# A two-layer decoder trunk: key stage begun later, last triangular inversion spread wider, bonus task later, recurrence hops closer

## The chip, the cores and the metric

The kernel runs on one core of one Trainium2 chip. The metric is the device time of one execution in microseconds (us). Three runs of the kernel before gave 2402.3, 2398.12 and 2408.5 us; their median, 2402.3 us, is the time that the change is held against. The profile was taken of one further execution.

Five engines have a queue of their own and work through it in order: PE (matrix products), DVE (elementwise), ACT (activation functions and copies), POOL (elementwise), and SP, which only issues transfers. PEld is the weight load of PE, which overlaps it.

## What is computed

Layer 0 is an attention with forget gates, layer 1 an RWKV-7 time mixing; each has a modulated norm ahead of it and a gated residual add behind it. The change lies in layer 1. Cut to what matters:

```python
xr, xw, xk, xv, xa, xg = (h + xx * mu[i] for i in range(6))     # xx = h shifted by one token, less h
r, k, v, z = xr @ w_in[0], xk @ w_in[1], xv @ w_in[2], xg @ w_in[3]
w_log = -softplus(-(w0 + tanh(xw @ w1) @ w2)) - 0.5             # low-rank stage: w, a, v
decay = exp(-exp(w_log))
v = v + (v_first - v) * sigmoid(v0 + (xv @ v1) @ v2)
a = sigmoid(a0 + (xa @ a1) @ a2)
kk = normalised(k * k_k);  k = k * (1 + (a - 1) * k_a)
# per head, token by token:  a_t = -kk, b_t = kk * a
S = S * w_t + (S a_t) b_t^T + v_t k_t^T ;   y_t = S r_t
y = groupnorm(y) * lnx_w + lnx_b + sum(r * k * r_k) * v         # the last term is the bonus
x = x + gate * ((y * silu(z)) @ w_out)
```

SEQ is 512, D_MODEL 2048, 32 heads of 64. All is float32; a large product is made of three passes over operands split into a high and a low part.

## The kernel before, in words

**The backbone.** Layer 1 has 74 dense tiles of PE work: 10 left of the keys, then 16 each of receptance (r), values (v), gate (z) and output projection. A tile is one PSUM bank of 128 x 512 outputs and takes 16 k-steps; a step is three matmuls, `pj<-hi,whi`, `pj<-hi,wlo`, `pj<-lo,whi`. Four k-steps use one weight group (256 KB): SP loads it as `raw`, ACT rounds it to `whi`, DVE makes `wlo`. There are three buffers for `raw` and four for `whi` and `wlo`.

**What sets the order.** Everything else runs as tasks: Python generators that emit instructions and then `yield` how much PE work is to pass before they go on. `Flow` (L108) keeps a clock that advances with every matmul emitted (a 128 x 512 matmul by 512/2400 = 0.213), and a heap of due tasks. So the numbers in `yield` fix where an instruction stands in each engine's queue. They set no time: on the chip an engine that reaches an instruction whose input isn't there waits, and all that stands behind it in its queue waits too.

**The side work of layer 1** (`side`, L1758) goes through a low-rank stage (`lora_k`, `lora_up`), then 16 `keys` tasks, one for each 128 rows of keys, KEY = 9.8 apart. A `keys` task loads `ip`, `kt` and `aa`, squares the keys on ACT (`sq<-kt`), splits the square (`mhi` on ACT, `mlo` on DVE) and sums it over a head on PE (`S<-mhi,blkr`, `S<-mlo,blkr`, in `means`, L1097); it goes on to the products that the chunks of 64 tokens need. After each four of them `invert` (L1388) inverts 32 x 32 triangles, 128 at once, in 30 steps of two operations (`lt<-lane`, `lane<-lane,lt`). The first three inversions run on POOL. The last one (group 3, DG) runs on DVE, its steps spread over DINV of PE work; its first step waits for the transfer `lane<-mld`. `inverse` follows DINV + 8 behind it. When all keys are through, the recurrence begins.

**The recurrence.** `stage` (L1477) loads for each of 16 pairs of chunks and makes `eI<-prk` on ACT; `products` (L1529) makes `L` and `GP`, and `recur` (L1590) takes one chunk after the other in three hops, each on the grid of HOP (`hop`, L1585): x from S and L, x from `xs` and `QP`, x from S and `tok`. `bonus` (L1569) is started 2 behind the end of a stage; it loads `vv`, and sums `prk` over a head with the same `means` as the keys (`mhi<-prk`, `mlo<-prk`). `normed` (L1646) norms the outcome of a pair of chunks, with `means` twice (`mhi<-ys`, `mhi<-sq`). All these products share two PSUM banks named S. `gated` multiplies with silu(z), and the output tiles need all of that.

Nearly all instructions pass through one recording helper, so that the profile shows them with its line, L90. They are told apart by the names of what they write and read.

Of the kernel before, what the change touches and what calls it, by code (L numbers as in the profile page):

```python
# [131 lines left out]
def body(ctx, tc, a, out, dbg=None, stop=0):  # L132
# [961 lines left out]
    def read(tag, n):  # L1094
        rings[tag][n] = fl.t + 0.7

    def means(q, w, x, th, tl):  # L1097
        hi = q.tile([P, T], R, tag=th, name="mhi")
        lo = q.tile([P, T], R, tag=tl, name="mlo")
        act_hi(hi, x)  # L1100
        yield 0.6
        dve.tensor_tensor(out=lo, in0=x, in1=hi, op=OP.subtract)
        yield 1.8
        n = yield from need("S")
        ss = bank("S")
        pe.matmul(ss, w, hi, start=True, stop=False)
        pe.matmul(ss, w, lo, start=False, stop=True)
        return ss, n

    def take(tag):  # L1110
        while not free[tag]:
            yield 0.2
        free[tag] -= 1
# [22 lines left out]
    def keep(j, o):  # L1136
        t = mq.tile([P, T], F, tag="z", name="kt")
        act.activation(t, o, AF.Copy)
        yield 1.5
        sp.dma_start(kTd[j], t)  # L1140
# [5 lines left out]
    def lora_k(q, k):  # L1146
        if k == 0:
            lb.extend(bank(t) for t in "SSy")
        hp = load(mq, h1d[k], "hp", (P, T + 1), bufs=NHP)
        raw = load(q, a["lora"][k], "rawl", (P, NL))  # L1150
        yield 4
        wh = q.tile([P, 1, NL], R, tag="whl", name="whl")
        wl = q.tile([P, 1, NL], R, tag="wll", name="wll")
        act_hi(wh[:, 0], raw)
        ns = (1, 4, 3)
        ms = [q.tile([P, T], F, tag=f"m{n}", name="m", bufs=1 + (n == 3)) for n in ns]
        d = q.tile([P, T], F, tag="d", name="d")
        pool.tensor_tensor(out=d, in0=hp[:, 0:T], in1=hp[:, 1:], op=OP.subtract)
        ts = [tuple(q.tile([P, T], R, tag=f"m{x}{n}", name="m" + x) for x in "hl") for n in ns]
        yield 1.4  # L1160
        for i in range(5):
            if i == 1:
                dve.tensor_tensor(out=wl[:, 0], in0=raw, in1=wh[:, 0], op=OP.subtract)
            if i < 3:
                dve.scalar_tensor_tensor(out=ms[i], in0=d,
                                         scalar=vecs[:, V_MU + ns[i], k:k + 1],
                                         in1=hp[:, 1:], op0=OP.mult, op1=OP.add)
            if 1 <= i < 4:
                act_hi(ts[i - 1][0], ms[i - 1])
            if 2 <= i:  # L1170
                e = pool if i - 2 < 1 else dve
                e.tensor_tensor(out=ts[i - 2][1], in0=ms[i - 2], in1=ts[i - 2][0],
                                op=OP.subtract)
            yield 0.7
        yield 1
        sp.dma_start(mxd[0, k], ms[2])
        premixed.add((0, k))
        for t, o, (m0, m1) in ((ts[i], lb[i], lspan[i]) for i in (1, 2, 0)):
            mm3(o[0:m1 - m0, :], (wh, wl), 0, t, k == 0, k == KT - 1, m0, m1)
            yield 1  # L1180
        if k == KT - 1:
            lb.append(None)
# [22 lines left out]
    def lora_w(q, g, n):  # L1205
        nm, rows = (("w2", LW), ("a2", LA_), ("v2", LV))[n]
        raw = load(q, a[nm][:, g * T:(g + 1) * T], "w2r", (rows, T), bufs=3)
        if n == 2:
            wh = q.tile([2 * LV, T], R, tag="v2h", name="v2h", bufs=2)
        else:  # L1210
            wh = q.tile([rows, T], R, tag="w2h", name="w2h", bufs=4)
            wl = q.tile([rows, T], R, tag="w2l", name="w2l", bufs=4)
        yield 6.5
        act_hi(wh[0:rows], raw)
        yield 1.2
        if n == 2:
            dve.tensor_tensor(out=wh[LV:], in0=raw, in1=wh[0:LV], op=OP.subtract)
        else:
            dve.tensor_tensor(out=wl, in0=raw, in1=wh, op=OP.subtract)
        yield 1.2  # L1220
        uw[g, n] = (wh,) if n == 2 else (wh, wl)
# [64 lines left out]
    def mixz(q, k):  # L1286

        yield from take("m")
        hp = load(mq, h1d[k], "hp", (P, T + 1), bufs=NHP)
        yield 5  # L1290
        m = q.tile([P, T], F, tag="mm", name="m", bufs=2)
        act.activation(m, hp[:, 1:], AF.Copy, scale=omu[:, 2, k:k + 1])
        yield 1.5
        dve.scalar_tensor_tensor(out=m, in0=hp[:, 0:T], scalar=vecs[:, V_MU + 5, k:k + 1],
                                 in1=m, op0=OP.mult, op1=OP.add)
        free["m"] += 1
        yield 1.5
        sp.dma_start(mxd[2, k], m)
        premixed.add((2, k))
# [267 lines left out]
        staged[m] = SV, L, qp, gp, dec, tok  # L1567

    def bonus(q, g, u, prk):  # L1569
        vv = q.tile([P, T], F, tag="vv", name="vv", bufs=1)  # L1570
        sp.dma_start(vv.rearrange("p (j t) -> p j t", j=NJ), vvd[g][:, u])
        yield 6
        yield from take("B")
        bo, n = yield from means(q, blkr, prk.rearrange("p j c t -> p (j c t)"), "mh", "ml")
        free["B"] += 1
        yield 0.9
        yield from take("bv")
        bv = q.tile([P, T], F, tag="bv", name="bv", bufs=2)
        dve.scalar_tensor_tensor(out=bv, in0=bo, scalar=float(DH), in1=vv, op0=OP.mult,
                                 op1=OP.mult)  # L1580
        read("S", n)
        free["prk"] += 1
        staged[g, u] = bv

    def hop():  # L1585
        n = fl.t // HOP
        while fl.t // HOP == n:
            yield 0.1
# [162 lines left out]


    STW = 5
    DG, DINV = (3,), 32
    HOP = 3.9
    INV, KEY = 54, 9.8

    def side(q):  # L1758
        for j, o in enumerate(ks):
            fl.start(0, keep(j, o))  # L1760
        for k in range(KT):
            fl.start(fl.t, lora_k(q, k))
            yield 5.2
        while len(lb) < 4:
            yield 0.2
        yield 0.5
        pools.close()
        q = pools.enter_context(tc.tile_pool(name="uq", bufs=2, reuse_waits="tile"))
        for n in range(3):
            fl.start(fl.t, lora_w(q, 0, n))  # L1770
        rmask = q.tile([P, NCH, C], F, name="rmask", bufs=1)
        pool.memset(rmask, 1.0)
        pool.memset(rmask[:, :, 0:1], 0.0)
        rms.append(rmask)
        lora_act(q)
        yield 3.5
        for j in range(KT):
            for n in range(3):
                if j % 4 == 0 and j < KT - 4:
                    fl.start(fl.t, lora_w(q, j // 4 + 1, n))  # L1780
                fl.start(fl.t, lora_up(q, j, n))
                yield 0.8
        while len(ups) < 3 * KT:
            yield 0.2
        yield 3
        pools.close()
        kp = pools.enter_context(tc.tile_pool(name="kp", bufs=1, reuse_waits="tile"))
        eIs.append(kp.tile([P, NCH, C + 1], F, name="eI"))
        for i in range(5):
            qts.append(kp.tile([P, NCH, C], F, name=f"qt{i}"))  # L1790
            for r in (32, 96):
                pool.memset(qts[i][r:r + 32, :, 0:32], 0.0)
        pool.memset(eIs[0][:, :, 0:1], 1.0)
        for j in range(KT):
            if "v" in dbg:
                print("keys", j, fl.t, len(ends))
            fl.start(fl.t, keys(kp, j))
            fl.start(fl.t + 5, mixz(kp, j))
            yield KEY
        while len(qd) < KT or len(premixed) < 3 * KT:  # L1800
            yield 0.2
        yield 3
        pools.close()
        rk = pools.enter_context(tc.tile_pool(name="rk", bufs=1, reuse_waits="tile"))
        for i in range(4):
            QP.append([rk.tile([P, NJ, C], F, name=f"QP{i}{h}") for h in range(2)])
            GP.append([rk.tile([P, NJ, C], F, name=f"GP{i}{h}") for h in range(2)])
            for h in range(2):
                pool.memset(QP[i][h][OS[h]], 0.0)
                pool.memset(GP[i][h][OS[h]], 0.0)  # L1810
        def stages():
            for n in range(NG * NU):
                g, u = divmod(n, NU)
                while any(NJ * g + i not in rd for i in range(NJ)):
                    yield 0.2
                yield from stage(rk, g, u)

        fl.start(fl.t, stages())
        fl.start(fl.t, recur(rk))

    fl.start(0, side(q))
    Av, Ar, Az, G = [], [], [], []
    ready = {(id(A), k) for k in range(KT)}
# [37 lines left out]
```

## Time and profile before

| | |
|---|---|
| median of three runs | 2402.3 us (2398.12 to 2408.5) |
| profiled execution: its time, its span | 2401.73 us, 2399.9 us |
| PE busy | 2302.2 us, 96% of the span |
| PEld, DVE, ACT, POOL busy | 75%, 67%, 52%, 29% |
| granted TensorE clock, mean | 0.982 |

Layer 1 fills about the last 1100 us. A row of a timeline begins with its start and its duration in us; what stands in brackets is how long the engine had been idle before it, and what ended that. A row of windows gives busy time and count for each engine, then the granted clock (PEclk), the busy share of the 16 DMA engines and GB/s.

### The profile page before, as it was taken

To read this page: it belongs to the slowest core of one execution; us is meant where nothing else is said; L and a number is where in the kernel's file an instruction comes from. 1 tells how busy PE (TensorE), PEld (TensorE's weight loads), DVE (VectorE), ACT (ScalarE), POOL (GpSimd) and SP (SyncE) were. 2 spreads that over 40 slices of the span, in tenths; PEclk is the share of its full clock that TensorE was granted. 3 is DMA by queue.
4 is the path that set the end of the run, shared out by engine and by line. 5 is a ranking of instruction groups with operands and counts; after the bars stand their busy time and mean duration, and the time that the engine had idled before them with its cause. 6 is when DMAs were issued, how large, how long until landed. Compare 5 with 4: busy or idle time off the path is not lost. (4 is left out here: it accounts for less than half of the span.)

```text
span 2399.9 us, 39413 instructions
## 1 busy us (share of the span) xinstructions
PE 2302.2 (96%) x13626; PEld 1807.3 (75%) x13626; DVE 1605.2 (67%) x2850; ACT 1256.5 (52%) x2300; POOL 694.4 (29%) x1114
## 2 busy tenths in 40 slices
PE   6999999999999999998999898899999899999999
PEld 4787777877778778886777676677777677777787
DVE  6886778888888635336797567666476776755322
ACT  4435655555565545225646777763345556665221
POOL 0002333442424210110141208771245535450000
PEclk8999999999999999999999999899999999999999
DMA  8864466766666346445756999886867766544543
GB/s 307 328 227 156 128 211 217 222 213 213 205 224 220 114 161 225 142 141 157 223 179 198 308 263 277 256 252 187 233 187 195 219 174 194 167 132 154 161 137 97
DMA packets 388152, 480.23 MB, mean 200 GB/s; under 512 B 146032, under 2 KB 217840, under 8 KB 384112
## 3 DMA queue, kind: packets, MB, share of 16 engines
q1 hardware_dynamic: 386288, 475.08, 63.7%
q0 software_dynamic: 1664, 2.63, 0.3%
q8 instruction: 108, 1.77, 0.3%
q14 instruction: 92, 0.75, 0.1%
HBM read 381.63 MB, written 95.95 MB: 199 GB/s over the span
## 5 line engine op out<-in xcount | busy, mean ns | idle before, releaser
L90 PE MATMUL pj<-hi,whi 128*128 128x512 f32 x2416 | 987.4, 409 | 11.0 <-ACT hi L90 8.2
L90 PE MATMUL pj<-hi,wlo 128*128 128x512 f32 x2416 | 959.4, 397 | 10.1 <-DVE wlo L90 10.0
L90 PE MATMUL pj<-lo,whi 128*128 128x512 f32 x2416 | 959.9, 397 | 0.0
L90 DVE TENSOR_TENSOR wlo<-raw,whi 128x512 fp32r<-128x512 f32 (+2 forms) x628 | 473.4, 761 | 255.1 <-ACT whi L90 252.4
L90 ACT ACTIVATE whi<-raw 128x512 fp32r<-128x512 f32 (+2 forms) x628 | 393.9, 634 | 399.0 <-PE pj L90 215.1
L90 PEld LDWEIGHTS pj<-hi,whi 128*128 128x128 f32 x2416 | 459.5, 190 | 116.8 <-ACT hi L90 9.2
L90 PEld LDWEIGHTS pj<-lo,whi 128*128 128x128 f32 x2416 | 458.3, 190 | 108.4 <-DVE lo L90 0.7
L90 PEld LDWEIGHTS pj<-hi,wlo 128*128 128x128 f32 x2416 | 459.9, 190 | 105.2 <-DVE wlo L90 13.4
L90 DVE CUSTOM_DVE_ANT_0 wm<-wm,cb 128x1024 f32<-128x1024 f32 x128 | 155.8, 1217 | 0.3
L90 POOL TENSOR_SCALAR SV<-SV,dec 64x64 f32<-64x64 f32 x224 | 94.2, 442 | 103.9 <-DVE SV L90 69.7
L90 ACT ACTIVATE pr<-Sm,mx 128x128 f32<-128x128 f32 (+3 forms) x128 | 71.5, 559 | 76.8 <-POOL mx L90 76.3
L90 POOL TENSOR_SCALAR pr<-pr,rc 128x128 f32<-128x128 f32 (+3 forms) x128 | 100.8, 788 | 26.0 <-DVE rc L90 23.6
L90 POOL TENSOR_SCALAR mx<-mx 128x1 f32<-128x1 f32 x128 | 59.9, 468 | 143.2 <-DVE mx L90 98.0
L90 DVE CUSTOM_DVE_ANT_0 Sm<-S,cmask 128x128 f32<-128x128 f32 (+3 forms) x128 | 62.3, 487 | 42.5 <-PE S L90 41.8
L90 POOL TENSOR_TENSOR lt<-lane 128x30 f32<-128x30 f32 (+14 forms) x90 | 64.2, 713 | 86.4 <-DMA lane<-mld 79.6
L90 POOL TENSOR_TENSOR bk<-bk,eI 128x512 f32<-128x512 f32 x32 | 36.6, 1142 | 110.3 <-PE S L90 64.0
L90 POOL TENSOR_TENSOR lane<-lane,lt 128x30 f32<-128x30 f32 (+14 forms) x90 | 64.0, 711 | 7.0
L90 PE MATMUL S<-k,q 128*128 128x128 f32 (+7 forms) x256 | 61.9, 323 | 0.0
L90 POOL TENSOR_TENSOR acc<-acc,sq 128x512 f32<-128x512 f32 x14 | 18.1, 1296 | 149.4 <-ACT sq L90 128.2
L90 ACT ACTIVATE pT<-tr 128x512 f32<-128x512 f32 x64 | 31.0, 485 | 54.4 <-PE tr L90 54.4
L90 DVE SCALAR_TENSOR_TENSOR hp<-pj,gate,hp 128x512 f32<-128x512 f32 x16 | 12.0, 751 | 68.0 <-PE pj L90 68.0
L90 PE MATMUL tr<-ident,pr 128*128 128x128 f32 x320 | 56.0, 273 | 1.5 <-DVE pT L90 1.3
(325 smaller groups left out, 3284.0 us busy)
## 6 DMA issues: line engine op xcount, KB each, us to landing
wm<-in_wmodT SPq DMA_DIRECT2D x132, 512.0 KB, 4.4
raw<-in_wz SPq DMA_DIRECT2D x128, 256.0 KB, 3.7
raw<-in_wo SPq DMA_DIRECT2D x128, 256.0 KB, 3.6
raw<-in_wv SPq DMA_DIRECT2D x124, 256.0 KB, 3.9
wm<-in_wmodT SPq DMA_DIRECT2D x30, 1024.0 KB, 6.4
raw<-in_wk SPq DMA_DIRECT2D x96, 256.0 KB, 3.7
raw<-in_wr SPq DMA_DIRECT2D x64, 256.0 KB, 5.0
raw<-in_wq SPq DMA_DIRECT2D x56, 256.0 KB, 3.5
```

The costliest lines, as they stand in the source:

```text
L90: self.last = f(*a, **k)
```

## The change

Four numbers of the plan change; no instruction is added or taken away.

```diff
     def bonus(q, g, u, prk):
+        yield 5
         vv = q.tile([P, T], F, tag="vv", name="vv", bufs=1)
...
     STW = 5
-    DG, DINV = (3,), 32
-    HOP = 3.9
+    DG, DINV = (3,), 40
+    HOP = 3.8
     INV, KEY = 54, 9.8
...
         while len(ups) < 3 * KT:
             yield 0.2
-        yield 3
+        yield 8
         pools.close()
         kp = pools.enter_context(tc.tile_pool(name="kp", bufs=1, reuse_waits="tile"))
```

What it moves shows in the order of each engine's instructions. In PE's order each of the 16 `S<-mhi,blkr` of the keys stands 21 to 30 `pj` matmuls later than before, 14 of them 21 or 24 later (24 are two weight groups, or half a tile). The matmuls behind the last inversion stand 51 later, the recurrence's first `x<-SV,L` also 51, and its last `y<-GP,SV` 9.

The first key on ACT, before (`kt<-pj` is the end of a backbone tile, `hi<-hp` the split of an activation for the next group of tiles):

```order
L90 ACTIVATE sq<-kt,vecs 128x512
L90 ACTIVATE eI<-ip 128x8x64
L90 ACTIVATE hi<-hp 128x512
L90 ACTIVATE kt<-pj 128x512
L90 ACTIVATE whi<-raw 128x512
L90 ACTIVATE hi<-hp 128x512
L90 ACTIVATE mhi<-sq 128x512
```

The same place of ACT after the change:

```order
L90 ACTIVATE kt<-pj 128x512
L90 ACTIVATE whi<-raw 128x512
L90 ACTIVATE hi<-hp 128x512 x2
L90 ACTIVATE kt<-pj 128x512
L90 ACTIVATE sq<-kt,vecs 128x512
L90 ACTIVATE eI<-ip 128x8x64
L90 ACTIVATE whi<-raw 128x512
L90 ACTIVATE m<-hp,omu 128x512
L90 ACTIVATE mhi<-sq 128x512
```

The square stands behind both `kt<-pj` now, and `mhi` follows it with less between them.

The start of the last inversion on DVE, before:

```order
L90 TENSOR_TENSOR lt<-lane 128x30
L90 TENSOR_TENSOR lane<-lane,lt 128x30
L90 TENSOR_TENSOR lo<-hp,hi 128x512
L90 TENSOR_TENSOR wlo<-raw,whi 128x512
L90 TENSOR_TENSOR lt<-lane 128x58
L90 TENSOR_TENSOR lane<-lane,lt 128x2x29
L90 TENSOR_TENSOR lt<-lane 128x84
L90 TENSOR_TENSOR lane<-lane,lt 128x3x28
L90 TENSOR_TENSOR lo<-hp,hi 128x512
L90 TENSOR_TENSOR lt<-lane 128x108
L90 TENSOR_TENSOR lane<-lane,lt 128x4x27
L90 TENSOR_TENSOR wlo<-raw,whi 128x512
```

After the change:

```order
L90 TENSOR_TENSOR lo<-hp,hi 128x512 x2
L90 TENSOR_TENSOR wlo<-raw,whi 128x512
L90 TENSOR_TENSOR lt<-lane 128x30
L90 TENSOR_TENSOR lane<-lane,lt 128x30
L90 TENSOR_TENSOR lt<-lane 128x58
L90 TENSOR_TENSOR lane<-lane,lt 128x2x29
L90 TENSOR_TENSOR lo<-hp,hi 128x512
L90 TENSOR_TENSOR wlo<-raw,whi 128x512
L90 TENSOR_TENSOR lt<-lane 128x84
L90 TENSOR_TENSOR lane<-lane,lt 128x3x28
L90 TENSOR_TENSOR wlo<-raw,whi 128x512
```

Between the first `wlo` behind the inversion's start and the next one there stood three steps and a `lo`, and there stands one step now.

The first `bonus` on ACT, before (`tok` and `vt` are copies out of the S banks):

```order
L90 ACTIVATE eI<-prk 128x512
L90 ACTIVATE whi<-raw 128x512
L90 ACTIVATE mhi<-prk 128x512
L90 ACTIVATE tok<-S 128x512
L90 ACTIVATE whi<-raw 128x512
```

After the change:

```order
L90 ACTIVATE eI<-prk 128x512
L90 ACTIVATE tok<-S 128x512
L90 ACTIVATE whi<-raw 128x512
L90 ACTIVATE vt<-S 128x512
L90 ACTIVATE tok<-S 128x512
L90 ACTIVATE mhi<-prk 128x512
```

`mhi<-prk` had one row between itself and the next stage's `eI<-prk`, and has four now.

## The prediction, made before the changed kernel ran

> **What bounds the kernel now.** I read the page first, then busy time by windows, then PE's waits, then the timeline around each wait.
>
> The page: span, busy time of the engines, and PE and its clock in 40 slices of 60 us.
>
> ```profile
> span 2399.9 us, 39413 instructions
> PE 2302.2 (96%) x13626; PEld 1807.3 (75%) x13626; DVE 1605.2 (67%) x2850; ACT 1256.5 (52%) x2300; POOL 694.4 (29%) x1114
> ...
> PE   6999999999999999998999898899999899999999
> PEclk8999999999999999999999999899999999999999
> ```
>
> PE is the bound. The change alters only how long PE stands idle and how long it runs at a lowered clock. Its first visible effect is the place of the first key, so I cut the time from there into windows.
>
> ```profile
> 1360.00:1380.00 20.00, 14.84 (x54) 11.42 (x53) 12.64 (x16) 15.64 (x28) 6.64 (x6) 0.83 0.91 299
> 1380.00:1600.00 220.00, 203.14 (x1397) 156.75 (x1396) 149.99 (x193) 158.00 (x295) 132.08 (x184) 0.95 0.91 261
> 1600.00:1650.00 50.00, 42.91 (x333) 33.07 (x332) 39.83 (x84) 21.60 (x42) 15.88 (x16) 0.86 0.66 205
> 1650.00:1730.00 80.00, 79.96 (x725) 63.98 (x723) 37.55 (x68) 30.59 (x62) 13.90 (x35) 1.00 0.84 226
> 1730.00:1745.00 15.00, 11.30 (x83) 8.65 (x84) 8.90 (x20) 5.63 (x11) 2.97 (x5) 0.89 0.77 203
> 1745.00:2190.00 445.00, 431.71 (x4264) 338.22 (x4261) 308.87 (x661) 255.49 (x439) 203.87 (x386) 0.99 0.62 176
> 2190.00:2240.00 50.00, 47.01 (x199) 36.63 (x198) 26.50 (x48) 24.55 (x40) 0.00 (x0) 1.00 0.63 197
> ```
>
> PE's idle time is the width less the first busy figure: 5.2 us at the first key, 16.9 in the rest of the key stage, 7.1 around the last inversion, 0 behind it, 3.7 at the first bonus, 13.3 in the recurrence, 3.0 at the end of the gate tiles. That is 49 us, and the lowered clock comes on top. All that the change can win lies in this, and it can add to it.
>
> **The change part by part.**
>
> *Keys 5 later.* The first key, PE and then ACT; the first two rows are the first and the last of 70 `pj` matmuls in a row.
>
> ```profile
> 1350.00 0.39 PE L90 MATMUL pj<-lo,whi 128*128 128x512 f32 x1
> ...
> 1366.04 0.39 PE L90 MATMUL pj<-lo,whi 128*128 128x512 f32 x1
> 1369.61 0.50 PE L90 MATMUL S<-mhi,blkr 128*128 128x512 f32 x1 [3.18 <-ACT mhi L90]
> 1372.09 0.79 PE L90 MATMUL S<-mlo,blkr 128*128 128x512 f32 x1 [1.99 <-DVE mlo L90]
> 1372.68 0.63 PE L90 MATMUL pj<-hi,whi 128*128 128x512 f32 x1
> 1373.11 0.63 PE L90 MATMUL pj<-hi,wlo 128*128 128x512 f32 x1
> ```
>
> ```profile
> 1365.77 0.71 ACT L90 ACTIVATE sq<-kt,vecs 128x512 f32<-128x512 f32 x1
> ...
> 1368.94 0.61 ACT L90 ACTIVATE mhi<-sq 128x512 fp32r<-128x512 f32 x1
> ...
> 1372.28 0.58 ACT L90 ACTIVATE kt<-pj 128x512 f32<-128x512 f32 x1
> ```
>
> PE's step is 16.04 us / 69 = 0.2325 us, so the 24 matmuls that now stand ahead are 5.6 us of work, and PE would come to the key at about 1371.9 instead of 1366.3. ACT is what it waits for. ACT's rows ahead of `mhi` in the new order are, but for one `whi`, those that ran up to `kt<-pj` at 1372.28; with that one, `mhi` ends near 1373.5, and `mlo`, which took 0.7 to 1.8 us behind it there, near 1374.2 to 1375.2. Half of the wait stays (2.3 to 3.3 us). Against 1372.09 PE is then 2.1 to 3.1 us late with 5.6 us more done: a gain of 2.5 to 3.5 us. Behind the wait a step took 0.43 instead of 0.23 us from 1372.1 for some 5 us (0.83 of the clock over 20 us), which cost 2.2; with a shorter wait it may not come. Bounds: nothing, and 5.2 + 2.2 = 7.4. I take 3, since the clock's part hangs on a gap that stays.
>
> *The other 15 keys.* PE's waits from 1380 to 1600:
>
> ```profile
> PE S L90 <- ACT mhi L90: 7.3, 4, 3.9
> PE S L90 <- DVE mlo L90: 6.4, 8, 1.2
> PE x L90 <- ACT us L90: 2.9, 4, 1.0
> ```
>
> They are the same two matmuls of later keys, and an inverse. The DMA engines are 0.91 busy there. Most of these keys move by two weight groups, so each meets the same piece of weight traffic as before, and each engine's order around it is nearly the same. I take 0, within 6 either way: each of these waits is on ACT behind a weight that landed late, and moves with the traffic. SP carries the keys' loads past two weight loads; nothing there waits for them sooner than PE.
>
> *The last inversion over 40.* DVE at its start, DVE from 1605 to 1649 in groups, DVE's share of the worst 30 us, and PE's waits from 1600 to 1650:
>
> ```profile
> 1605.52 0.19 DVE L90 TENSOR_TENSOR lt<-lane 128x30 f32<-128x30 f32 x1 [10.04 <-DMA lane<-mld]
> ```
>
> ```profile
> L90 DVE TENSOR_TENSOR lt<-lane 128x30 f32<-128x30 f32 (+14 forms) x30 | 16.2, 540 | 10.5 <-DMA lane<-mld 10.0
> L90 DVE TENSOR_TENSOR lane<-lane,lt 128x30 f32<-128x30 f32 (+14 forms) x30 | 10.0, 332 | 1.0
> L90 DVE TENSOR_TENSOR wlo<-raw,whi 128x512 fp32r<-128x512 f32 x12 | 9.3, 777 | 1.3 <-ACT whi L90 1.3
> L90 DVE TENSOR_TENSOR lo<-hp,hi 128x512 fp32r<-128x512 f32 x8 | 5.5, 685 | 0.0
> ```
>
> ```profile
> 1610.00:1640.00 30.00, 24.75 (x145) 19.18 (x146) 29.08 (x55) 11.78 (x21) 8.98 (x6) 0.82 0.66 196
> ```
>
> ```profile
> PE pj L90 <- DVE wlo L90: 7.1, 3, 2.8
> ```
>
> Here DVE is the bound for a while: 29.08 of 30 us busy, and PE waits for `wlo`. The inversion's 60 operations take 16.2 + 10.0 = 26.2 us. Planned over 32 they have 32 / 0.2133 x 0.2325 = 34.9 us, which is 75% of DVE. A `wlo` of 0.777 us for each 12 matmuls (2.79 us) is 28%, the eight `lo` in 44 us 12%: 115%, more than there is. Over 40 they have 43.6 us, 60%, and the sum is 100%. So the two later waits, which come of the overflow (7.1 less the longest, 2.8, leaves 4.3 us), should go or nearly go. The longest comes behind the 10.0 us in which DVE stood still for `lane<-mld`, and that stays; only the order behind it is kinder to `wlo`. The clock was 0.82 over these 30 us, 5.4 us lost at most, part of it inside the waits; some 3 of it hang on the two later waits. I take 4.3 + 3 = 7; bounds 0 (the waits come as before at other places) and 7.1 + 5.4 = 12.5.
>
> ```profile
> 1630.00:1640.00 10.00, 6.88 (x76) 5.12 (x77) 9.63 (x21) 2.24 (x5) 1.55 (x1) 0.64 0.47 126
> ```
>
> In these 10 us, with waits of under 2.8 us each, the granted clock fell to 0.64. [...]
>
> *The bonus 5 later.* PE and ACT at the first bonus:
>
> ```profile
> 1737.01 0.49 PE L90 MATMUL S<-mhi,blkr 128*128 128x512 f32 x1 [3.46 <-ACT mhi L90]
> ```
>
> ```profile
> 1735.81 0.63 ACT L90 ACTIVATE whi<-raw 128x512 fp32r<-128x512 f32 x1 [3.08 <-DMA raw<-in_wv]
> ```
>
> `mhi<-prk` stood in ACT behind a weight that landed late; PE reached the sum 3.5 us too soon. In the new order it again stands behind a `whi`, with three short copies more between, so that the wait is a matter of which weight is late. Bounds: 3.7 us and 0.11 x 15 = 1.7 of clock gained, or as much lost at another of the 16 bonuses; I take a gain of 1.5, less than half of 3.7. Queued behind the moved load of `vv` on SP nothing new waits: `vv` has 6 units to land as before, and the second buffer of `prk` isn't wanted before the next stage but one.
>
> *Hops of 3.8, and the recurrence 51 matmuls later.* PE's waits from 1745 to 2190:
>
> ```profile
> PE S L90 <- ACT GP L90: 9.7, 5, 5.3
> PE x L90 <- DVE SV L90: 1.2, 2, 0.9
> ```
>
> A hop is 0.11 us shorter, and the chain's own waits (`DVE SV`) are 1.2 us in 32 chunks; should each of 96 hops have lost its slack this would show in more than two waits. I cost it at 0 to +1. The start 51 matmuls (11.9 us) later costs nothing, because the backbone fills PE meanwhile (79.96 of 80 us busy from 1650 to 1730). The end is 9 matmuls or 2.1 us later against the gate tiles. Late next would be the last `ypd`, and with it the output tiles. The waits at that place, 2190 to 2240:
>
> ```profile
> PE pj L90 <- DVE wlo L90: 2.9, 3, 1.5
> ```
>
> are for weights, not for the recurrence; bounds 0 and +2.1, I take +1, the middle.
>
> *Sum*: -3 (first key) - 0 - 7 (inversion) - 1.5 (bonus) + 0 + 1 (end) = -10.5, from the profiled 2401.7 to **2391 us**. The profiled execution lies 0.6 us under the median of 2402.3, so nothing is to be shifted.
>
> **Rivals.**
>
> *All the waits of the sums shrink.* The keys' 16.9 us and the recurrence's 9.7 come of PE reaching a sum before ACT has made its high part. If the later places suit ACT in general, a third of them goes with its clock, about 9 us, and the bonus's 3.7 whole: some 2380 (2374 to 2385). For it: the new order has `mhi<-prk` further from `eI<-prk`. Against it: for the keys both PE and ACT move together.
>
> *The transfers are the bound in the key stage, and what is won at the first key and at the inversion is given back.* For it: 0.91 busy over 220 us. Against it: behind the stage DMA falls to 0.66. Then only the slower clock's part is saved: 2397 to 2407, most likely 2400.
>
> *Slower: ACT stuck behind a stage's load.* This has happened once at full size, PE and ACT:
>
> ```profile
> 1919.39 0.79 PE L90 MATMUL S<-mhi,blkr 128*128 128x512 f32 x1 [5.28 <-ACT GP L90]
> ```
>
> ```profile
> 1917.31 0.63 ACT L90 ACTIVATE eI<-prk 128x512 f32<-128x512 f32 x1 [4.09 <-DMA prk<-ipd]
> ```
>
> `eI<-prk` waited 4.1 us for its load, `GP` behind it in ACT came late out of the S bank, and PE stood 5.3 us, with a slow stretch behind it (0.43 for 0.23 us in 3.6 us, 1.6). One such wait costs 6.9. The recurrence meets other transfers at all 16 stages now. Two more of them than before eat the forecast (2391 + 13.8 = 2405), and from there it is slower; four give 2419. Against it: only one of 16 stages had it.
>
> **How the numbers follow.** The forecast, 2385 to 2397 around 2391, has 0.47; the wider gain 0.20; the gain given back 0.23; slower than before by new waits 0.10. A measurement of this kernel tells about 0.5% from no change, 12 us: below 2390.3 is faster, above 2414.3 slower. Faster: all of the wider gain and somewhat under half of the forecast, 0.41. Slower: the waits' case with three or more of them, 0.07. The same: 0.52. The range leaves out the last of the wider gain and the case of new waits: 2375 to 2406.
>
> **What would show it.** PE's waits by window: from 1360 to 1380 about half of 5.2 us; around the last inversion one wait for `wlo` instead of three, DVE under 95% busy there and the clock above 0.9; no more than one wait of over 3 us in the recurrence; between the recurrence's end and the output tiles 3 to 5 us idle. I am wrong if the inversion's waits stay with DVE less busy (then the late weights are their cause), if the other keys' 16.9 us changes by more than 6, or if the recurrence has new waits behind `eI`.

## The result: 1.3% slower, and the profile after

The changed kernel takes 2433.7 us (median, 2430.2 to 2436.1) against 2400.3 us for the kernel before on the same chip (four runs of each): 1.013 times as long, with a 95% interval of 1.011 to 1.015. The forecast was 2391 us, its range ended at 2406, and slower had a chance of 0.07. The profiled execution took 2430.2 us.

First the page of the kernel after: the span, busy time, and PE and its clock in 40 slices.

```profile
span 2428.5 us, 39383 instructions
PE 2309.6 (95%) x13626; PEld 1811.8 (75%) x13626; DVE 1598.5 (66%) x2850; ACT 1256.4 (52%) x2301; POOL 692.0 (28%) x1114
PE   6999999999999999998999998889999899998999
PEclk9999999999999999999999999899999999999999
```

The work is the same, 13626 matmuls. Of PE's eights that at 1320 us, where the first key lay, is gone, and two are new, in the slices that begin near 1579 and 2186 us (a slice is 60.7 us now). To see what each stage cost, both traces were cut at the same places of PE's work, counted in backbone matmuls (`pj`): first key, other keys, last inversion, recurrence with its first stages and bonuses, and what follows the last chunk. The first cut, at the 4,210th, lies behind the first key's sums in both. The columns are those of the earlier windows. Before:

```profile
1250.00:1382.20 132.20, 122.15 (x501) 93.33 (x500) 91.79 (x112) 90.22 (x154) 29.37 (x33) 0.97 0.78 249
1382.20:1603.30 221.10, 204.24 (x1459) 157.58 (x1458) 147.83 (x189) 158.79 (x296) 134.77 (x190) 0.95 0.91 262
1603.30:1675.70 72.40, 65.31 (x550) 51.14 (x549) 52.52 (x107) 30.17 (x60) 14.06 (x12) 0.91 0.69 201
1675.70:2191.50 515.80, 498.76 (x4780) 391.35 (x4779) 343.31 (x726) 282.15 (x490) 219.87 (x423) 0.99 0.65 182
2191.50:2399.90 208.40, 201.55 (x862) 161.63 (x860) 71.22 (x113) 56.99 (x91) 0.00 (x0) 1.00 0.47 145
```

After:

```profile
1248.40:1377.00 128.60, 121.35 (x502) 92.57 (x501) 86.85 (x104) 86.77 (x149) 30.85 (x33) 0.99 0.79 249
1377.00:1597.10 220.10, 202.91 (x1396) 155.94 (x1394) 152.56 (x198) 159.31 (x296) 129.75 (x183) 0.96 0.90 259
1597.10:1668.60 71.50, 63.04 (x550) 49.73 (x550) 47.17 (x101) 31.27 (x63) 16.30 (x19) 0.93 0.75 229
1668.60:2215.20 546.60, 511.31 (x4843) 399.26 (x4842) 342.00 (x730) 283.70 (x494) 217.12 (x423) 0.97 0.62 172
2215.20:2428.50 213.30, 202.79 (x862) 163.28 (x860) 71.80 (x114) 57.53 (x92) 0.00 (x0) 0.98 0.46 141
```

The first key's stretch is 3.6 us shorter, about as forecast; the other keys and the inversion are 1.0 and 0.9 us shorter, which is next to nothing. From the start of the fourth stretch to the end it is 759.9 instead of 724.2 us: 35.7 us lost. Of these, 21.9 are idle time of PE (45.8 instead of 23.9, the widths less the busy figures) and 13.8 are PE's own busy time. Some 1.6 us of that are 64 small matmuls of the last inversion, which stood ahead of the cut before; the other 12 or so go with the lower clock (0.97 and 0.98 instead of 0.99 and 1.00): with both traces cut into windows of 4 us, PE's busy time times what the clock lacked of 1.00 adds up to 15.1 us after and 3.3 before. The loss lies where the forecast had costed the change at about nothing.

At the first key PE no longer waits for either sum. It waits a little ahead of them, for a copy of the backbone (`kt`) out of its bank:

```profile
1370.46 0.50 PE L90 MATMUL pj<-hi,whi 128*128 128x512 f32 x1 [2.16 <-ACT kt L90]
1373.32 0.71 PE L90 MATMUL S<-mhi,blkr 128*128 128x512 f32 x1
```

PE's waits in the recurrence of the kernel after, by what it waited for (us in total, times, longest):

```profile
PE S L90 <- DVE mlo L90: 17.2, 12, 2.9
PE x L90 <- DVE xs L90: 3.8, 1, 3.8
PE S L90 <- ACT GP L90: 3.8, 4, 2.7
PE S L90 <- ACT tok L90: 3.7, 1, 3.7
```

The 9.7 us behind `GP` have shrunk to 3.8. In their place stand twelve waits for a low part, all of a bonus. One of them, ACT's high part, DVE's queue up to the low part, and PE:

```profile
1821.83 0.62 ACT L90 ACTIVATE mhi<-prk 128x512 fp32r<-128x512 f32 x1
```

```profile
1820.65 2.31 DVE L90 SCALAR_TENSOR_TENSOR dc<-dc,vecs,sq 128x128 f32<-128x128 f32 x4
1822.89 1.13 DVE L90 SCALAR_TENSOR_TENSOR dc<-dc,vecs,bv 128x128 f32<-128x128 f32 x4
1823.94 0.70 DVE L90 SCALAR_TENSOR_TENSOR prk<-rt,vecs,bk 64x128 f32<-64x128 f32 x2
1824.66 0.69 DVE L90 TENSOR_TENSOR wlo<-raw,whi 128x512 fp32r<-128x512 f32 x1
1825.27 1.43 DVE L90 SCALAR_TENSOR_TENSOR prk<-rt,vecs,bk 64x128 f32<-64x128 f32 x4
1826.71 0.59 DVE L90 COPY L<-rt 64x256 f32<-64x256 f32 x2
1827.33 0.69 DVE L90 TENSOR_TENSOR mlo<-prk,mhi 128x512 fp32r<-128x512 f32 x1
```

```profile
1824.73 0.39 PE L90 MATMUL S<-mhi,blkr 128*128 128x512 f32 x1
1828.07 0.50 PE L90 MATMUL S<-mlo,blkr 128*128 128x512 f32 x1 [2.94 <-DVE mlo L90]
1829.07 0.49 PE L90 MATMUL pj<-hi,wlo 128*128 128x512 f32 x1
```

`mhi` was there at 1822.45, `mlo` began at 1827.33, 4.9 us later, though DVE was never idle: it worked off the next stage's `prk` and `dc`, among which the later bonus now stands. Over the 16 bonuses the median delay from the end of `mhi` to the start of `mlo` is 0.3 us before and 3.3 after. The plan allows the sum 1.8 units behind `mlo`, about 2 us of PE's steps.

The clock in windows of 4 us behind this wait and behind a shorter one:

```profile
1829.00:1833.00 4.00, 4.00 (x40) 3.01 (x39) 2.72 (x6) 0.60 (x1) 1.39 (x5) 0.57 0.11 24
1976.00:1980.00 4.00, 4.00 (x12) 3.15 (x11) 3.33 (x8) 0.00 (x0) 0.00 (x0) 0.57 0.56 144
```

```profile
1975.58 0.50 PE L90 MATMUL S<-mlo,blkr 128*128 128x512 f32 x1 [1.77 <-DVE mlo L90]
```

PE was busy throughout and the granted clock was 0.57: behind a wait of 2.94 us, and behind one of 1.77 us. Stretches like these make up most of the 13.8 us.

Near the first bonus, where PE had stood 3.46 us for `mhi`, it now stands about as long for `tok`, which ACT again copies behind a weight that landed late. PE and ACT:

```profile
1745.66 1.09 PE L90 MATMUL S<-ident,bk 128*128 128x128 f32 x4 [3.73 <-ACT tok L90]
```

```profile
1743.75 0.63 ACT L90 ACTIVATE whi<-raw 128x512 fp32r<-128x512 f32 x1 [5.37 <-DMA raw<-in_wv]
```

At the inversion of the kernel after, PE's waits, DVE at the start, and the worst 30 us:

```profile
PE pj L90 <- DVE wlo L90: 8.0, 2, 6.1
```

```profile
1610.86 0.19 DVE L90 TENSOR_TENSOR lt<-lane 128x30 f32<-128x30 f32 x1 [10.06 <-DMA lane<-mld]
```

```profile
1612.00:1642.00 30.00, 26.02 (x155) 20.30 (x156) 28.98 (x59) 10.68 (x19) 6.69 (x5) 0.85 0.63 186
```

DVE stands still as long as before, and then is as full as before: 28.98 of 30 us. The three waits became two, and the first of them, right behind the standstill, is 6.1 us long.

Behind the last chunk, DVE and PE:

```profile
2235.07 0.69 DVE L90 TENSOR_TENSOR z<-z,yp 128x512 f32<-128x512 f32 x1 [4.94 <-DMA yp<-ypd]
2239.19 0.69 DVE L90 TENSOR_TENSOR z<-z,yp 128x512 f32<-128x512 f32 x1 [3.42 <-DMA yp<-ypd]
2240.40 0.69 DVE L90 TENSOR_TENSOR wlo<-raw,whi 128x512 fp32r<-128x512 f32 x1
```

```profile
2241.14 0.80 PE L90 MATMUL pj<-hi,wlo 128*128 128x512 f32 x1 [6.71 <-DVE wlo L90]
```

The weight's `wlo` waits behind `z`, which waits for the last rows of `yp`.

### The profile page after: what moved, and what is told of

Read it like the earlier page. It is cut to its first block, busy times and chain, and to the rows that moved or that the text cites. A ratio compares the mean times of both kernels' runs of the same rounds, so it can differ in the third digit from the quotient of the medians.

```text
span 2428.5 us, 39383 instructions
## 1 busy us (share of the span) xinstructions
PE 2309.6 (95%) x13626; PEld 1811.8 (75%) x13626; DVE 1598.5 (66%) x2850; ACT 1256.4 (52%) x2301; POOL 692.0 (28%) x1114
## 3 DMA queue, kind: packets, MB, share of 16 engines
q8 instruction: 108, 1.77, 0.3%
## 5 line engine op out<-in xcount | busy, mean ns | idle before, releaser
L90 ACT ACTIVATE L<-S 64x512 f32<-64x512 f32 x64 | 37.5, 586 | 41.9 <-PE S L90 40.6
```

The lines of the kernel that those rows point to most:

```text
L90: self.last = f(*a, **k)
```

## The experiments

Two theories were to be told apart. A: the later bonus puts its low part behind other work in DVE's queue, and PE waits for it. B (B' where it is told of the place itself): the recurrence stands at another place of the backbone, and its many short products meet inputs that are not there yet. "Place" is counted from PE's order: how many backbone matmuls later than before the first and the last chunk stand; the change makes it 51 and 9. For the inversion, E is the standstill behind the load, F too much work for DVE.

The table has all runs. The stretch is the one from the 5,090th backbone matmul to the end, where the change lost its 35.7 us; idle is the stretch less PE's busy time in it. Where the last inversion ends later, 64 of its small matmuls, some 1.6 us, fall into the stretch as well (5704 instead of 5640); in e16_place_early 64 are missing. In the profiles whose recurrence keeps its place and has no new waits (e6, e7, e8, e10, e11) the stretch is 722.6 to 728.0 us, so that some 4 us tell nothing. The ratio is to the kernel before on the same chip, with its 95% interval.

| kernel | place, first/last | us | ratio | stretch | PE busy | idle |
|---|---|---|---|---|---|---|
| before | 0/0 | 2400.3 | 1 | 724.2 | 700.3 | 23.9 |
| after | 51/9 | 2433.7 | 1.013 [1.011, 1.015] | 759.9 | 714.1 | 45.8 |
| e1_no_bonus | 54/27 | 2429.1 | 1.011 [1.009, 1.013] | 753.9 | 713.4 | 40.5 |
| e2_bonus_alone | 0/0 | 2420.5 | 1.008 [1.007, 1.010] | 742.9 | 707.0 | 35.9 |
| e3_keys_alone | 18/18 | 2421.2 | 1.009 [1.007, 1.010] | 743.9 | 709.3 | 34.6 |
| e4_dinv_alone | 39/36 | 2424.2 | 1.010 [1.008, 1.012] | 751.8 | 710.8 | 41.0 |
| e5_hop_alone | 3/-42 | 2411.9 | 1.005 [1.003, 1.006] | 737.4 | 706.1 | 31.3 |
| e6_bonus_sum_later | 0/0 | 2402.3 | 1.000 [0.999, 1.001] | 722.7 | 699.7 | 23.0 |
| e7_keys_closer | 0/0 | 2403.5 | 1.001 [0.999, 1.002] | 722.6 | 700.3 | 22.3 |
| e8_load_ahead | 0/0 | 2399.5 | 0.999 [0.998, 1.000] | 727.8 | 705.1 | 22.7 |
| e9_change_sum_later | 51/9 | 2414.9 | 1.005 [1.004, 1.007] | 739.8 | 706.2 | 33.6 |
| e10_bonus_and_load | 0/0 | 2401.6 | 1.000 [0.999, 1.001] | 724.9 | 700.7 | 24.2 |
| e11_three_parts_in_place | 0/0 | 2404.5 | 1.002 [1.001, 1.003] | 728.0 | 702.8 | 25.2 |
| e12_sum_later_hop3p7 | 51/-3 | 2414.0 | 1.005 [1.004, 1.006] | 739.0 | 711.7 | 27.3 |
| e13_place_18 | 18/18 | 2414.3 | 1.005 [1.003, 1.007] | 740.2 | 708.0 | 32.2 |
| e14_place_36 | 39/36 | 2421.0 | 1.009 [1.007, 1.010] | 748.4 | 708.9 | 39.5 |
| e15_place_54 | 51/54 | 2421.4 | 1.009 [1.006, 1.011] | 746.6 | 707.2 | 39.4 |
| e16_place_early | -12/-18 | 2422.9 | 1.010 [1.007, 1.012] | 732.3 | 701.9 | 30.4 |

### The parts one by one

**The change without its bonus part.**

```diff
     def bonus(q, g, u, prk):
-        yield 5
         vv = q.tile([P, T], F, tag="vv", name="vv", bufs=1)
```

> All of the change but the later bonus. In the profile after the change PE waits 17 us in 12 of 16 bonus sums for the low part (mlo<-prk on DVE), against 1.3 us before. Theory A (the later bonus puts this low part behind DVE's burst for the next stage and the norm): the waits for it fall under 3 us, the time to 2390 to 2405 us. Theory B (the recurrence as a whole meets other work since it begins 51 matmuls later and its hops are closer; the waits would sit on other rows without the bonus): 2420 us or more, with as many PE waits in the recurrence as after the change (32 us).

2429.1 us, only 4.5 less than with it. `mlo` is in time again (0.35 us behind `mhi` in the median), but the stretch is still 753.9 us long, with its place at 54/27; PE now waits for other inputs of the S banks (`vf` 7.9 us, `tok` 6.5). A alone is not the cause.

**The bonus part alone**, on the kernel before.

```diff
     def bonus(q, g, u, prk):
+        yield 5
         vv = q.tile([P, T], F, tag="vv", name="vv", bufs=1)
```

> The kernel before, and of the change only the later bonus. Theory A: waits of 12 us or more for mlo<-prk in the recurrence and a time of 2420 to 2435 us. Theory B: under 5 us of such waits, 2395 to 2408 us.

2420.5 us: A is real. Nearly all products of the chunks stand where they stood (the others within 6 matmuls), and PE's waits in the recurrence have the change's signature:

```profile
PE S L90 <- DVE mlo L90: 15.8, 12, 2.7
PE S L90 <- ACT GP L90: 8.6, 4, 4.4
```

**The other three parts alone**, each on the kernel before.

```diff
-        yield 3
+        yield 8
         pools.close()
         kp = pools.enter_context(tc.tile_pool(name="kp", bufs=1, reuse_waits="tile"))
```

> The kernel before, and of the change only the keys' later start. Theory A: the gain at the first key stands alone and is kept, 2393 to 2400 us. Theory B: the recurrence, which begins later, loses more than that, 2408 us or more.

```diff
-    DG, DINV = (3,), 32
+    DG, DINV = (3,), 40
```

> The kernel before, and of the change only the last inversion over 40 instead of 32. Theory A: 2394 to 2404 us, with the three waits for weights around the inversion changed by less than 4 us. Theory B: 2406 us or more, lost in the recurrence. The prediction's own term, 7 us gained at the inversion, would give 2395.

```diff
-    HOP = 3.9
+    HOP = 3.8
```

> The kernel before, and of the change only the closer hops. Its recurrence begins where it did and ends 42 backbone matmuls earlier. Theory B' (the recurrence was fitted to its place; each other place costs 12 to 20 us of new waits on whatever it meets there): 2408 to 2420 us, with the loss in the recurrence; and because its end is early, the wait for weights ahead of the output tiles stays under 4 us. Theory D (what costs is only that the recurrence ends late against the output tiles): 2395 to 2403 us.

2421.2, 2424.2 and 2411.9 us: each part alone is slower. The four losses, 20 (bonus), 20, 23 and 11 us, add up to 74, more than twice the 33 of the whole. The keys' and the inversion's edits touch nothing in the recurrence but its place, and still lost 20 and 28 us in the stretch behind them.

The spread over 40 alone is also the plain test of the forecast's 7 us at the inversion. DVE is less busy there, 27.4 instead of 29.1 of the 30 us from 1610, but PE's waits have hardly shrunk from 7.1 us:

```profile
PE pj L90 <- DVE wlo L90: 5.9, 4, 2.6
```

### Undoing the two mechanisms

**The bonus's sum behind its low part.** The bonus is later as in the change, and its sum on PE waits 2.5 units longer.

```diff
-    def means(q, w, x, th, tl):
+    def means(q, w, x, th, tl, late=1.8):
...
-        yield 1.8
+        yield late
         n = yield from need("S")
...
     def bonus(q, g, u, prk):
+        yield 5
...
-        bo, n = yield from means(q, blkr, prk.rearrange("p j c t -> p (j c t)"), "mh", "ml")
+        bo, n = yield from means(q, blkr, prk.rearrange("p j c t -> p (j c t)"), "mh", "ml", 4.3)
```

> As with the later bonus alone (2420 us), but PE's two sums of the bonus stand a further 2.5 of PE work behind the low part. Theory A (PE comes to the sum while DVE still works off the next stage's and the norm's operations): the 15.8 us of waits for the low part fall under 5 us and the time to 2400 to 2410 us. If instead the later bonus costs by the load it puts on DVE, the waits move to other rows and the time stays at 2415 us or more.

2402.3 us: the bonus's 20 us are gone. `mlo` is no earlier than in the bonus part alone (2.9 against 2.1 us behind `mhi` in the median), but PE no longer stands in front of it; of the 15.8 us there remain

```profile
PE S L90 <- DVE mlo L90: 0.2, 1, 0.2
```

**Keys later, and closer together.** The keys begin 5 later and follow 9.5 instead of 9.8 apart, so that the recurrence stands where it stood.

```diff
-    INV, KEY = 54, 9.8
+    INV, KEY = 54, 9.5
...
-        yield 3
+        yield 8
         pools.close()
         kp = pools.enter_context(tc.tile_pool(name="kp", bufs=1, reuse_waits="tile"))
```

> The keys begin 8 behind the low-rank stage as in the change, but follow each other at 9.5 instead of 9.8, so that every matmul of the recurrence stands where it stood before the change. Theory B' (the place of the recurrence is what costs): the recurrence and the tail take what they took before (449 and 208 us of the trace), and the gain at the first key (8 us up to there) stays in part: 2391 to 2401 us. If a later start of the keys costs in itself, by transfers that are late afterwards: 2408 us or more as with the keys' later start alone (2421).

2403.5 us: with the place held the loss is gone (stretch 722.6 instead of 743.9). The gain that was expected did not come: the first key's stretch is 129.6 instead of 132.2 us, and the other 15 keys, closer together, take as much back (223.8 instead of 221.1). Over all runs, keys 8 behind take 128.6 to 130.5 us for the first stretch, keys 3 behind 131.5 to 133.7, so a gain of some 3 us there is real. With keys 9.8 apart nothing shows that the others give it back: they take 217.2 to 223.9 us, whether they begin 3 or 8 behind.

**The inversion begun behind its load.** The operations start 7 later, when `lane<-mld` has landed, and end where they ended.

```diff
         sp.dma_start(m, mld[grp])
+        if grp in DG:
+            yield 7
...
-                yield DINV / 30
+                yield (DINV - 7) / 30
```

> The kernel before, but the last inversion's first step on DVE stands 7 of PE work behind the issue of its load, and its steps are spread over the 25 that remain; the recurrence's place is untouched. Theory E (PE's waits around the inversion come of DVE's standstill of 10 us behind the load): they fall from 7.1 to under 4 us, 2392 to 2398 us. Theory F, the prediction's (they come of DVE having more work than time): over 25 the inversion is denser, so they grow to 9 us or more, 2402 to 2410 us.

2399.5 us. PE's waits at the inversion:

```profile
PE pj L90 <- DVE wlo L90: 4.5, 2, 3.2
```

They fell from 7.1 to 4.5 us though the operations are packed closer, over 25 instead of 32; in six other kernels that leave the inversion and the keys as they were they are 5.5 to 7.6. F said that they would grow, and it falls with this run. E has the right sign, but neither its waits of under 4 us nor its time was reached, so the standstill explains only a part of them. It is worth little: single profiles of that stage differ by 3 us with nothing changed in it (69.3 to 72.4), and the whole kernel is 1.3 us faster, at the edge of what can be told.

### Putting them together

**The whole change with the bonus's sum later** (the `means` edit above, on the changed kernel).

```diff
-        bo, n = yield from means(q, blkr, prk.rearrange("p j c t -> p (j c t)"), "mh", "ml")
+        bo, n = yield from means(q, blkr, prk.rearrange("p j c t -> p (j c t)"), "mh", "ml", 4.3)
```

> The whole change, with one thing more: the two sums of a bonus on PE stand 2.5 units further behind its low part (4.3 instead of 1.8). The recurrence still begins 51 backbone matmuls later than before. Theory A and B (two separate causes: the bonus's low part is late in DVE's order, and the recurrence at its new place meets other weights at the wrong moment): the waits for mlo in the recurrence fall from 17.2 us to under 5, the kernel gains about the 18 us that the same edit won on the bonus alone, and the other half of the loss stays: 2410 to 2420 us. Rival, theory A alone (the bonus is the whole cause; the place does nothing by itself once the bonus waits no more): 2396 to 2404 us. Rival, theory B alone (place sets the loss, the bonus's waits only take the place of others): 2428 to 2436 us.

2414.9 us, 18.7 less than the change: by this run A accounts for a little over half of the loss, and the rest stays with the place. The shares hang on the way in which a part is undone: without the bonus's 5 (the first experiment) only 4.5 us came back, with the recurrence at 54/27. PE's waits for `mlo` fell to

```profile
PE S L90 <- DVE mlo L90: 2.1, 2, 1.9
```

**The same with hops of 3.7**, so that the recurrence ends 3 matmuls sooner instead of 9 later.

```diff
-    HOP = 3.8
+    HOP = 3.7
```

> The whole change with the bonus's sums 2.5 later, and hops of 3.7 instead of 3.8, so that the recurrence begins 51 backbone matmuls later than before but ends 3 sooner. It parts the late end from the late begin. Theory T (the late end costs: the last chunks' output tiles come 9 matmuls late and DVE waits for their loads ahead of weights): the tail behind the recurrence shrinks from some 213 to 207 us, and the kernel is 4 to 7 us faster than the same with hops of 3.8. Rival (what the recurrence meets on its way sets its loss, hops closer together only meet other weights): no gain or a loss, within 5 us of the same with hops of 3.8, or slower.

2414.0 us, no gain. What follows the last chunk did shrink, from 212.6 to 208.1 us, and the recurrence, from the 5,300th backbone matmul to the 6,390th, took 3.1 of it back (467.9 against 464.8). The later end costs, but an earlier one bought by closer hops is in the main paid for on the way.

**Three parts with the place held**: keys 8 behind and 9.5 apart, the inversion behind its load, the bonus and its sum later.

```diff
+        yield 5    # bonus; its sums 4.3 behind the low part
...
-    INV, KEY = 54, 9.8
+    INV, KEY = 54, 9.5
...
-        yield 3
+        yield 8    # ahead of the keys
...
+            yield 7    # invert, behind the load; then (DINV - 7) / 30
```

> Three parts of the change at once (keys 8 behind the low-rank stage, the last inversion spread differently, the bonus 5 later), but with the recurrence held at its old place: keys 9.5 instead of 9.8 apart, the inversion's operations 7 behind their load over 25 units, hops of 3.9; and the bonus's sums 2.5 further behind their low part. Theory A and B: with the place held and the low part in time nothing of the loss is left: 2396 to 2406 us, recurrence 447 to 455 us, mlo waits in it under 3 us. Rival (the parts hurt together in a way that none does alone): 2412 us or more.

2404.5 us: 30 of the 33 us are gone, and the stretch is within 4 us of before, with two of the three parts in it as the change has them (keys 8 behind, bonus 5 later).

**The bonus and the inversion of these alone** (without the keys), as a candidate for a faster kernel.

```diff
+        yield 5    # bonus; its sums 4.3 behind the low part
...
+            yield 7    # invert, behind the load; then (DINV - 7) / 30
```

> Kernel before, with the bonus task 5 later and its sums 2.5 further behind the low part, and the last inversion's operations begun 7 later behind its load (over 25 instead of 32 units, so that it ends where it ended). The recurrence stands where it stood before. The candidate for a faster kernel. If the two edits add: the inversion's waits 4.5 to 5.1 instead of 7.1 us, the first bonus's wait of 3.5 us for mhi gone, no new waits for mlo: 2394 to 2400 us. Rival (what is won in one stage is given back in the next, as in the earlier runs): 2400 to 2404 us, not to be told from before.

2401.6 us, not to be told from before: the two small gains don't add up to one that a measurement shows.

### The place by itself

Until here each kernel that moved the recurrence moved something else too. One number ahead of the recurrence moves it alone.

```diff
-        yield 3
+        yield 4.3    # 8.12, 13.24
         pools.close()
         rk = pools.enter_context(tc.tile_pool(name="rk", bufs=1, reuse_waits="tile"))
```

> Kernel before, with one number changed: 4.3 instead of 3 units between the last key task and the recurrence, so that stages, bonuses and chunks all stand 18 backbone matmuls later, and nothing else moves. Theory P (the place alone costs): 2416 to 2424 us, as the keys begun later gave with the same 18. Rival M (the loss of that run came of the key stage and its loads moving, not of the place of the recurrence): 2397 to 2405 us.

> The same with 8.12 instead of 3: 36 backbone matmuls later (39 at the first chunk). If any place but the old one costs about the same: 2416 to 2426. If the cost goes with the distance: twice that of 18, 2432 to 2442. If the phase against the weight groups (12 matmuls each) decides, 36 is three whole groups and costs only its late end: 2400 to 2408.

> The same with 13.24 instead of 3: 54 backbone matmuls later (51 at the first chunk), as the whole change has it at its first chunk. If any place but the old one costs about the same: 2416 to 2428, a little over 18 later for the later end. If the cost goes with the distance: 2445 or more. If the phase decides, 54 stands as 18 does: the same as that within 5 us.

> Kernel before with keys 9.5 instead of 9.8 apart: the recurrence stands 12 (first chunk) to 18 matmuls earlier, the inversion 24 earlier. If only a later place costs: 2392 to 2402. If any place but the old one costs: 2408 to 2422, with the loss in the recurrence's waits. The key stage may lose up to 3 us by itself.

2414.3, 2421.0, 2421.4, and 2422.9 for the early one (keys 9.5 apart). In the order of the three later places and the early one, the stretch by windows:

```profile
1671.10:2411.30 740.20, 708.00 (x5640) 558.12 (x5638) 412.28 (x839) 340.41 (x581) 222.38 (x423) 0.98 0.59 167
```

```profile
1669.90:2418.30 748.40, 708.85 (x5640) 561.08 (x5638) 408.32 (x840) 344.44 (x586) 221.52 (x423) 0.98 0.58 166
```

```profile
1669.60:2416.20 746.60, 707.15 (x5640) 559.46 (x5638) 413.05 (x839) 344.20 (x583) 223.94 (x423) 0.98 0.59 166
```

```profile
1688.40:2420.70 732.30, 701.92 (x5576) 553.63 (x5574) 408.70 (x840) 339.20 (x577) 225.09 (x423) 0.99 0.60 169
```

The same backbone took 16.0, 24.2, 22.4 and 8.1 us longer than before. So the place alone costs: 11.3, 18.0 and 18.4 us of the whole kernel at 18, 36 and 54. That is more than rival M allowed and, at 18, less than the 2416 us at which P began. The keys begun later had cost 20 us at the same 18, though the chunks' products stand in the same places there. Its stretch is nearly as long (743.9 us, with the 64 small matmuls); 4.2 us of the rest lie at the last inversion. Of e13's 16.0 us only 11.3 show in the whole kernel: in its profile the time ahead of the stretch is 4.6 us shorter, 3.1 of them at the inversion, which is as much as single profiles of that stage differ by.

Twice or three times the distance doesn't cost twice or three times as much, nor does 36, three whole weight groups, come out cheaper than 18 or 54: of the three expectations "any place but the old one" fits best. The loss has two parts. Up to the 6,390th backbone matmul it is 9.3, 12.1 and 8.6 us, whatever the distance; behind it 6.7, 12.0 and 13.8 us, more the later the recurrence ends (at 54 the last chunk itself stands behind that cut).

The early kernel is a weaker witness. Only 8.1 us of its loss lie in the stretch; 13.0 were lost in the key stage (234.1 against 221.1 us), where at most 3 had been expected. PE's waits for `mlo` there are 12.3 instead of 6.4 us. Keys as close together but begun later took only 223.8 us in the kernel with the place held, so for the keys, too, the place counts.

What PE waits for at the new places is no one thing. In the recurrence of the kernel 36 later:

```profile
PE S L90 <- ACT vt L90: 6.3, 2, 3.4
PE S L90 <- DVE vf L90: 4.8, 3, 2.4
PE x L90 <- issue: 3.2, 1, 3.2
PE S L90 <- ACT GP L90: 2.7, 4, 1.7
```

And behind the last chunk, one wait grew with the later end: 5.7 us at 18, 6.6 at 36, and at 54

```profile
PE pj L90 <- ACT z L90: 10.9, 1, 10.9
```

Open is what singles out the old place. The products of a chunk stand in fixed order among weights on ACT and DVE, and any shift pairs them anew with weights that land late; that this pairing was good at the old place, by luck or by choice, fits all runs, but none shows it.

## Why the prediction was wrong, step by step

- **The place, "costs nothing, because the backbone fills PE meanwhile": this step failed.** The backbone did fill PE from 1645 to 1725 (78.6 of 80 us), and that was not the question. Every product of the 32 chunks now stands beside other weights, and moving the recurrence alone cost 11 to 18 us. The forecast had bounded the start and the end of the recurrence, and not the 450 us between. Why the old place is the cheap one stays open.
- **The bonus, -1.5 within 5.4 either way: failed too.** Alone it cost 20 us, in the whole change 18.7. The forecast followed the high part on ACT at the first bonus, where before showed a wait. It did not follow the low part on DVE, which had no wait to show: 0.3 us behind `mhi`. And it bounded one bonus where 16 are moved. The first bonus's wait of 3.5 us for `mhi` went, but one of 3.7 for `tok` came near it, as the forecast's own "a matter of which weight is late" allowed; and twelve waits of up to 2.9 us for `mlo` came.
- **Hops, 0 to +1:** +11 alone, with the last chunk 42 matmuls sooner. The recurrence took 16 us more, and behind the last chunk 4.4 were won. Closer hops also shift each chunk against the weights; how much of the 16 comes of that and how much of the shorter hop itself is not shown.
- **The later end, +1 within 2.1: mis-sized.** With 9 matmuls more the part behind the last chunk took 4.9 us more. The forecast weighed the delay itself, 2.1 us, and left out that DVE's queue holds a weight's `wlo` behind `z` (PE stood 6.71 us for it), and the slow clock behind that wait (0.50 in 4 us). With the recurrence alone moved, what stands behind the 6,390th matmul took 6.7 to 13.8 us more for an end 18 to 54 matmuls later.
- **The first key, -3 within 0 and -7.4, and the other keys, 0: right in size.** The first stretch is 3.6 us shorter, the other keys' 1.0. `mhi` ended at 1373.2 us, near the 1373.5 of the forecast. But PE did not stand there for it: the waits for both sums are gone, and the 2.2 us that stayed are a wait for `kt`, which the forecast had not seen. That it came out at half of 5.2 us was luck.
- **The inversion, -7: wrong.** 0.9 us came, within what the stage varies by. The sum of 115% and then 100% took DVE's load as spread evenly. But DVE first stands still for 10 us behind `lane<-mld`, and at 100% there is no room to work off what has queued meanwhile; in the kernel after the share stayed at 97%. With the spread alone it fell to 91%, and PE still waited 5.9 us: the forecast's own sign of being wrong, waits that stay with DVE less busy. With the steps begun behind the load they fell to 4.5. What makes the rest of the waits is not shown.
- **The rivals.** The slower one had the right sign and another mechanism: no waits of `GP` behind `eI` came, on the contrary these fell from 9.7 to 3.8 us. That gains are given back was not seen at the first key. That all waits shrink was not, either.
- **The clock: right.** The forecast counted slower work beside waits of under 2.8 us, by its row of 0.64. After the change the clock was 0.57 to 0.59 in the 4 us behind four waits of 1.77 to 2.67 us, and some 12 of the lost 35.7 us went with a lower clock.

## What to carry over

In an order that is written down ahead, a later task is costed by what it newly stands behind on every engine's queue, for each of its repetitions, also where the trace shows no wait now: look up how long before its use each operand is ready, and compare that with the shift. Where a stage of many short steps is moved against a stream of weights, take the spread of a few shifts (here 11 to 18 us for 18 to 54 matmuls) as the bound of its cost, not nothing. When stages are compared, see that each cut has the same work ahead of it: a cut at the 4,190th matmul would put the first key into one stage before and into the next after, and show a gain of 8 us where there are 4. If a producer gets later, move its consumer along: 2.5 units more ahead of the bonus's sum took back all of its 20 us.

## What the runs showed of the hardware

In the kernel after, from the end of the last inversion on, PE stood 17 times for 0.8 us or more. In the 4 us from the matmul that ended the wait the granted clock was 0.50 to 0.64 behind the eight waits of 1.77 to 6.71 us, and 1.00 behind the nine of 0.82 to 1.55 us. In the kernel before it was 0.70 and 0.55 behind the waits of 3.46 and 5.28 us, and 1.00 behind the other five, one of them of 1.92 us. In the stretch behind the inversion each us of idle time that the change added came with some 0.6 us of slower work (about 12 to 21.9, the 64 small matmuls taken off).
